# Two transformer blocks in one Trainium2 kernel: feed-forward columns of both token streams joined, attention heads paired, projections reordered, and the last layer's norm taken in token blocks

## The chip, the cores and the metric

The kernel runs on one core of one Trainium2 chip. The metric is the device time of one execution in microseconds (us), as the median over several runs. A TensorE matmul instruction here multiplies a stationary tile (loaded by a weight load) with a moving tile of up to 512 columns; VectorE (DVE), ScalarE (ACT) and GpSimd (POOL) do everything else, and SyncE (SP) issues most transfers.

## The reference

The input is 256 tokens of width 1024, and a context of another 256 tokens. A first block of two layers runs on the tokens alone (retention and stick-breaking attention, then a gated feed-forward with 2816 hidden columns). A second block of two layers runs on both, with shared weights:

```python
x = first_block(x, ...)
h = ctx
for l in range(2):
    x = ffn_sublayer(x, mod_x, 0, *f0)      # adaptive norm, swiglu, adaptive norm, residual
    h = ffn_sublayer(h, mod_h, 0, *f0)      # the same weights
    ax, ah = adaln_in(x, ...), adaln_in(h, ...)
    uv, qb, qc, kb, vb, kc, vc = split(ax @ w_in[l])   # for ah too; in the last layer only kb, vb, kc, vc
    o_a = chunk_gmlp(uv, ...)                          # gated token mixing
    o_b = diff_attention(qb, [kb_h, kb_x], [vb_h, vb_x])   # 4 heads, two softmaxes each
    o_c = windowed_attention(qc, kc, vc, kc_h, vc_h, sink) # 4 heads on 2 key heads
    x = adaln_out(x, concat(o_a, o_b, o_c) @ w_out[l], ...)   # h too, but not in the last layer
    x = ffn_sublayer(x, mod_x, 2, *f1)                        # h too, but not in the last layer
return x
```

Everything is float32. The modulation vectors mod_x and mod_h come from a product with w_mod (1024 x 9216 per layer).

## The kernel before

**Products in three passes.** A float32 product is made from two halves: a value is split into a high part, rounded to a shorter format (fp32r), and the rest, its low part. A product is high x high + high x low + low x high, three matmuls. A weight granule of 1024 columns per partition comes by DMA into a `raw` tile; `split` writes its high part on ScalarE (`A.copy`) and its low part on VectorE (`V.tensor_sub`), in two pieces each, into an `hl` tile, of which there are five. The activations' parts are tiles `y` (before a projection), `a` (inside the feed-forward) and `o` (the mixer's output), high part written by ScalarE, low part by VectorE after it. `mm3` issues the three matmuls of one contraction step next to each other, and `proj` calls it for each of the eight steps of a column pair.

**Streams and a planner.** The program is a list of units in five streams: `sx` (the tokens, called X), `sh` (the context, H), `sat` (attention), `smod` (modulation vectors on VectorE) and `stot`. `run` is a planner at build time: it picks, by costs and classes in tables (`PE_NS`, `CLASS`), which unit's instructions are emitted next, so the order on each engine's queue is fixed when the kernel is built, and each engine executes its queue in order.

**Feed-forward.** `ffn` has 22 columns j of 128 hidden units. `col(j)` makes gate and up of one column for one stream in one bank of PSUM (tile `mm_c`, 48 matmuls of 256 moving columns, one for each pass, step and matrix), then SiLU, product and split. `row(s)` multiplies two hidden columns with w_down into 1024 outputs (24 matmuls of 512 columns; tile `mm_r` where H adds in SBUF, `mm_f` where X keeps sums in PSUM). In block 2 the streams X and H run beside each other and share most weight granules; each has its own `col`.

**Mixer of block 2.** `attn2` makes the projections (`kb0`, `kb1`, `vb`, `kcvc`, `v`, `qb0`, `u`, `qb1`, `qc`, in this order) and the attention items: for each differential head and each half of the tokens two score matmuls (`at_s`), softmax (VectorE maximum, ScalarE exponential, VectorE scaling of `p`), transposes (`at_t`) and a value product (`at_o`); the windowed heads have one score matmul for each item on 64 rows of the array (`v` selects the rows) and a value product `at_c` on 64 output columns. `bapply` and `gm` finish the mixer's parts, and `row_units` multiplies with w_out. `post_units` adds to the residual (`res`) what was scaled by an inverse root mean square, `pre_units` normalises (`z`), transposes (`mm_y`) and writes `y`. Nearly every instruction is recorded at the helper's line 205, so the rows below are told apart by their tiles.

## Time and profile before

| | |
|---|---|
| median of 3 runs | 2468.3 us (2467.7 to 2470.83) |
| the profiled execution | 2468.97 us, of which the profile's span is 2467.1 us |
| TensorE | 2409.6 us busy (98%), 16543 matmuls, mean granted clock 0.993 |
| VectorE, ScalarE | 1727.6 us (70%), 1094.3 us (44%) |
| chain that ended last | TensorE 88%, VectorE 8% |

A busy TensorE is not TensorE at its peak: the end of a matmul in the profile is modelled, and a group's time is best read from the start of one group to the start of the next. A granted clock of 1.00 is 2.4 GHz and of 0.50 is 1.2 GHz; values between are a mix over the stretch.

### The profile page before, as it was taken

The page shows a single profiled execution, that of the slowest core. Times are in us where ns is not written, and L with a number is a line of the kernel's source. Part 1 is how long each engine was busy: PE and PEld are TensorE (multiplying, and loading weights), DVE is VectorE, ACT ScalarE, POOL GpSimd, SP SyncE. Part 2 cuts the span into 40 slices and gives each one's busy share as a digit, 9 for nine tenths or more (in the row PEclk, how much of TensorE's full clock was granted, in tenths as well). Part 3 has the DMA queues.
Part 4 walks back from the last instruction along what each step waited for, and adds up shares of the span by engine and source line. Part 5 has one row for each costly group of instructions (what it writes and reads, how often), then busy time and mean ns, then how long its engine had stood idle before and what let it go on. Part 6 is the DMA issues. An engine that isn't in the chain of part 4 may idle for free.

```text
span 2467.1 us, 41782 instructions
## 1 busy us (share of the span) xinstructions
PE 2409.6 (98%) x16543; PEld 2211.5 (90%) x16543; DVE 1727.6 (70%) x3366; ACT 1094.3 (44%) x2331; POOL 99.3 (4%) x189
## 2 busy tenths in 40 slices
PE   8999999999999999999999999999999999997998
PEld 7999999999999999989669999999999999866997
DVE  5789667798789933756688994348998448486554
ACT  6654456545532222636465222236322226465443
POOL 1000000010011000000000100000110000000000
PEclk9999999999999999999999999999999999999999
DMA  7568655686667533522226652245675335322663
GB/s 228 165 209 263 179 168 158 191 267 194 205 188 210 167 98 90 178 88 84 62 94 205 214 180 86 86 120 188 206 213 154 95 87 181 93 86 78 190 193 120
DMA packets 455301, 386.26 MB, mean 157 GB/s; under 512 B 20512, under 2 KB 380260, under 8 KB 455104
## 3 DMA queue, kind: packets, MB, share of 16 engines
q1 hardware_dynamic: 431280, 299.67, 41.0%
q0 software_dynamic: 23648, 83.77, 10.7%
q8 instruction: 130, 2.13, 0.4%
q14 instruction: 67, 0.55, 0.1%
q10 hardware_dynamic: 176, 0.14, 0.0%
HBM read 382.43 MB, written 1.10 MB: 155 GB/s over the span
## 4 chain that ended last, share of the span: by engine, by line
PE 88%; DVE 8%; ACT 1%; DMA 1%; issue 1%; DVEq 0%; ACTq 0%
PE mm_c L205 57%; PE mm_f L205 17%; PE mm_r L205 6%; DVE hl L205 2%; PE at_s L205 2%; PE mm_t L205 1%; DVE res L205 1%; PE at_o L205 1%; DVE fo L205 1%; PE at_t L205 1%; DMA raw<-in_w_in_dram 1%; DVE t L205 1%; PE at_c L205 1%; PE st_rb L205 1%; DVE rs_t L205 1%
## 5 line engine op out<-in xcount | busy, mean ns | idle before, releaser
L205 PE MATMUL mm_c<-y,hl 128*128 128x256 f32 x11616 | 1436.4, 284 | 10.4 <-DVE y L205 7.5
L205 PEld LDWEIGHTS mm_c<-y,hl 128*128 128x128 f32 x11616 | 1418.8, 192 | 23.8 <-DVE y L205 8.8
L205 ACT CAST hl<-raw 128x512 fp32r<-128x512 f32 x1128 | 649.0, 619 | 814.5 <-PE mm_c L205 445.3
L205 DVE TENSOR_TENSOR hl<-raw,hl 128x512 fp32r<-128x512 f32 x1128 | 733.2, 685 | 339.4 <-ACT hl L205 338.3
L205 PE MATMUL mm_f<-hl,a 128*128 128x512 f32 x1584 | 381.5, 393 | 0.0
L205 PEld LDWEIGHTS mm_f<-hl,a 128*128 128x128 f32 x1584 | 291.5, 188 | 57.6
L205 DVE SCALAR_TENSOR_TENSOR modacc<-modraw,sc,modacc 128x1024 f32<-128x1024 f32 x252 | 311.6, 1277 | 0.0
L205 ACT ACTIVATE sg<-mm_c 128x256 f32<-128x256 f32 x154 | 58.6, 381 | 311.0 <-PE mm_c L205 307.5
L205 PE MATMUL mm_r<-hl,a 128*128 128x512 f32 x792 | 190.5, 392 | 0.0
L205 DVE TENSOR_TENSOR sg<-sg,mm_c 128x256 f32<-128x256 f32 x154 | 64.0, 416 | 154.0 <-ACT sg L205 153.2
L205 PEld LDWEIGHTS mm_r<-hl,a 128*128 128x128 f32 x792 | 145.2, 188 | 28.0
L205 PE MATMUL mm_f<-hl,o 128*128 128x512 f32 x480 | 119.3, 399 | 0.0
L1000 POOL DMA_DIRECT2D modraw<-in_w_mod_dram x144 | 77.3, 538 | 991.6 <-DVE modacc L205 625.8
L205 PE MATMUL mm_c<-hl,y 128*128 128x512 f32 (+1 forms) x528 | 108.7, 363 | 0.0
L205 PEld LDWEIGHTS mm_f<-hl,o 128*128 128x128 f32 x480 | 87.8, 189 | 23.1 <-issue 4.6
L205 PEld LDWEIGHTS mm_c<-hl,y 128*128 128x128 f32 x528 | 88.8, 189 | 14.7 <-issue 0.3
L205 DVE TENSOR_TENSOR fo<-fo,mm_r 128x512 f32<-128x512 f32 x120 | 81.6, 682 | 9.2 <-PE mm_r L205 8.5
L205 ACT CAST a<-sg 128x256 fp32r<-128x256 f32 x154 | 62.5, 406 | 30.1 <-DVE sg L205 30.0
L205 DVE TENSOR_TENSOR a<-sg,a 128x256 fp32r<-128x256 f32 x154 | 64.4, 418 | 8.5 <-ACT a L205 8.5
L205 DVE TENSOR_TENSOR gu<-mm_c,rfac 128x512 f32<-128x512 f32 x44 | 30.3, 688 | 48.7 <-PE mm_c L205 48.6
L205 DVE TENSOR_REDUCE sx<-at_s 128x1 f32<-128x512 f32 (+1 forms) x72 | 40.8, 596 | 26.3 <-PE at_s L205 25.7
L205 DVE TENSOR_REDUCE modt<-mm_t 128x4 f32<-128x512 f32 x72 | 49.2, 684 | 8.4 <-PE mm_t L205 8.2
(196 smaller groups left out, 1412.4 us busy)
## 6 DMA issues: line engine op xcount, KB each, us to landing
modraw<-in_w_mod_dram POOLq DMA_DIRECT2D x144, 512.0 KB, 4.7
raw<-in_ffn_w_down_dram SPq DMA_DIRECT2D x100, 512.0 KB, 4.4
raw<-in_ffn_w_gate_dram SPq DMA_DIRECT2D x98, 512.0 KB, 4.7
raw<-in_ffn_w_up_dram SPq DMA_DIRECT2D x98, 512.0 KB, 3.9
raw<-in_w_in_dram SPq DMA_DIRECT2D x92, 512.0 KB, 4.7
raw<-in_w_gate_dram SPq DMA_DIRECT2D x44, 512.0 KB, 4.9
raw<-in_w_up_dram SPq DMA_DIRECT2D x44, 512.0 KB, 5.1
raw<-in_w_down_dram SPq DMA_DIRECT2D x44, 512.0 KB, 4.9
```

What stands on the lines that cost most here:

```text
L205: return f(*args, **kw)
L1000: G.dma_start(M["raw"][g % len(M["raw"])], wm[k * P:(k + 1) * P, i * D:(i + 1) * D])
```

## The change

1. **Joint columns.** In the two feed-forwards of block 2's first layer and in the first one of its last layer, columns 2 to 19 (first feed-forward) or 4 to 19 (second) are made for both streams at once: `both(j)` has a unit for gate and one for up, each with 24 matmuls whose moving operand is `yy[:, :, part, k, :]`, 2 x 256 columns in two runs. `y`, and the mixer's output, now lie in one tile `yy` for both streams. That is 52 columns.
2. **Paired heads.** A windowed-attention item now takes two heads (`v` = 0 and 1) that lie on different 64 rows of the array in the scores and on different 64 output columns in the value product, whose matmuls alternate. w_out's rows for this part are loaded in a matching order.
3. **Mixer reordered.** The projections' order is the table `SEQ`; `bapply` and `gm` have places of their own, `gm` now after the last attention item; w_out's parts come as 1, 2, 3, 0; more buffers for transposed weights (`wt`, 4).
4. **Low part last.** `proj` now makes three passes over the steps: high x high, weights' low x high, and the activations' low part last.
5. **Last layer by token blocks.** The last two parts of w_out run for token block 0 and then for block 1; norm, residual and `z` are made for each block by itself, the gate is multiplied into a tile `fg` beside the squares (`beside`), and the first four weight granules of the last feed-forward get their low part on GpSimd (`by_pool`).
6. Modulation in block 1 uses the buffers of block 2's (`mod_buf2`), and the scratch for GpSimd's transfers is set to 8192.

```diff
+SEQ = ("kb0 kb1 qb0 vb qb1 kcvc qc v u".split(),
+           "kb0 kb1 vb qb0 qb1 kcvc qc v u".split())
...
+    PASSES = ((0, 0), (1, 0), (0, 1))
...
     def proj(ps, gs, y, ks=range(KT)):
-        for k in ks:
-            for m, g in enumerate(gs):
-                mm3(ps[:, m, :], wsl(g, 0, k, 0, P), wsl(g, 1, k, 0, P), y[:, 0, k, :], y[:, 1, k, :],
-                    k == 0 and m == 0, k == KT - 1 and m == 1)
+        for wp, yp in PASSES:
+            for k in ks:
+                for m, g in enumerate(gs):
+                    PE.matmul(ps[:, m, :], wsl(g, wp, k, 0, P), y[:, yp, k, :],
+                              start=k == 0 and m == 0 and wp + yp == 0, stop=k == KT - 1 and m == 1 and yp == 1)
...
+        def both(j):
+            box = {}
+            def part(g, ps):
+                for wp, yp in PASSES:
+                    for k in range(KT):
+                        PE.matmul(ps, wsl(g, wp, k, 0, P), yy[:, :, yp, k, :],
+                                  start=k == 0 and wp + yp == 0, stop=k == KT - 1 and yp == 1)
...
+            ug = st.add("joint", gate, grans=[gg[j]], deps=dep if j == 0 else ())
+            cols[j] = joint[1][j] = st.add("joint", up, grans=[gu[j]])
...
                     yield A
+                    if beside:
+                        if gated[0] is None:
+                            gated[0] = wk.tile([P, 2, D], F32, tag="A1", name="fg")
+                        def mul():
+                            yield V
+                            fo[c][b][e] = gated[0][:, b, e * 512:(e + 1) * 512]
+                            V.tensor_mul(fo[c][b][e], f, ctab[c][:, e * 512:(e + 1) * 512])
+                        meter.spawn(mul())
                     sq_piece(c, b, e, f)
...
+        for g in range(2):
+            for b in range(2):
+                def sc(g=g, b=b):
+                    pt = ptile()
+                    pss = [at_ps([P, 512], "at_s") for _ in range(2)]
+                    for v in range(2):
+                        PE.matmul(pss[v][:, :n], B["qc"][v * 64:v * 64 + 64, g, b * P:(b + 1) * P],
                                   K2["kc"][v * 64:v * 64 + 64, 0:n], start=True, stop=True)
...
+                    for j in range(nk):
+                        for v in range(2):
+                            PE.matmul(ps[v * 64:v * 64 + 64, :S], K2["vc"][:, j, v * 64:v * 64 + 64],
+                                      B["wtc", g][v][:, j, :], start=(j == 0), stop=(j == nk - 1))
...
+        pieces = (1, 2, 3, 0) if GM_AT[l] >= 12 else (1, 2, 0, 3)
...
+            for i in range(N_POOL):
+                for part in f1[:2]:
+                    part[i].by_pool = True
...
+            for n_ in range(4 - 2 if last else 4):
+                u = piece(n_)
+            for b in range(2 if last else 0):
+                for n_ in range(4 - 2, 4):
+                    u = piece(n_, (b,))
...
-        yield V
-        V.tensor_sub(g.hl[:, 1, c], r[:, c], g.hl[:, 0, c])
+        yield GP if g.by_pool else V
+        (GP if g.by_pool else V).tensor_sub(g.hl[:, 1, c], r[:, c], g.hl[:, 0, c])
```

On TensorE, in the second feed-forward of block 2's first layer, the queue before has two columns of one stream (`y_13964` is X's input, `y_13452` H's; `a_13667` and `a_14155` are the hidden columns of H and X), then rows, then a column of the other.

```order
L205 MATMUL mm_r<-hl,a_13667 128x512 x12
L205 MATMUL mm_c<-y_13964,hl 128x256 x96
L205 MATMUL mm_r<-hl,a_13667 128x512 x12
L205 MATMUL mm_f<-hl,a_14155 128x512 x6
L205 MATMUL mm_c<-y_13452,hl 128x256 x48
L205 MATMUL mm_f<-hl,a_14155 128x512 x18
L205 MATMUL mm_c<-y_13452,hl 128x256 x48
```

The same place in the changed kernel, where `yy` is the input of both streams and `a_12732` and `a_13210` are H's and X's hidden columns:

```order
L210 MATMUL mm_r<-hl,a_12732 128x512 x24
L210 MATMUL mm_c<-yy,hl 128x512 x24
L210 MATMUL mm_f<-hl,a_13210 128x512 x24
L210 MATMUL mm_c<-yy,hl 128x512 x72
L210 MATMUL mm_r<-hl,a_12732 128x512 x24
```

Two columns of both streams were 192 matmuls of 256 columns and are now 96 of 512; the rows are the same in number. Over the whole program 4,992 matmuls of 256 columns are replaced by 2,496 of 512.

On TensorE, where the last layer's attention of X begins before (`k_21693` are keys, `at_21912` holds the queries, `kr` and `at_r` the rotation of a projection):

```order
L205 MATMUL at_s<-k_21693,at_21912 128x512 x4
L205 MATMUL mm_c<-y_21857,hl 128x256 x48
L205 MATMUL at_s<-k_21693,at_21912 128x512 x2
L205 MATMUL at_t<-cst,p 128x128 x4
L205 MATMUL at_s<-k_21693,at_21912 128x512 x2
L205 MATMUL mm_c<-y_21857,hl 128x256 x24
L205 MATMUL at_t<-cst,p 128x128 x4
L205 MATMUL at_r<-kr,tab_c_6411 128x256 x4
L205 MATMUL at_s<-k_21693,at_21912 128x512 x2
L205 MATMUL at_t<-cst,p 128x128 x4
```

And in the changed kernel:

```order
L210 MATMUL at_s<-k_19011,at_19237 128x512 x4
L210 MATMUL mm_c<-yy,hl 128x256 x24
L210 MATMUL at_r<-kr,tab_c_6412 128x256 x2
L210 MATMUL at_s<-k_19011,at_19237 128x512 x2
L210 MATMUL mm_c<-yy,hl 128x256 x24
L210 MATMUL at_t<-cst,p 128x128 x4
L210 MATMUL at_s<-k_19011,at_19237 128x512 x2
L210 MATMUL mm_c<-yy,hl 128x256 x24
L210 MATMUL at_t<-cst,p 128x128 x4
```

Between the first scores and the last transposes there were 72 projection matmuls (`mm_c`, 256 columns) and 18 of w_out (`mm_f`, 512 columns); now there are 168 and none, and all 96 of w_out come after the attention.

On VectorE, at the norm between the last mixer and the last feed-forward, the queue before adds to the residual for both blocks and has four weight pieces (`hl`) between:

```order
L205 SCALAR_TENSOR_TENSOR rs_t<-rs_a,rs_t 128x2
L205 SCALAR_TENSOR_TENSOR res_78<-mm_f,rs_t,res_78 128x512 x3
L205 TENSOR_TENSOR hl<-raw,hl 128x512 x2
L205 SCALAR_TENSOR_TENSOR res_78<-mm_f,rs_t,res_78 128x512
L205 TENSOR_TENSOR hl<-raw,hl 128x512 x2
L205 SCALAR_TENSOR_TENSOR rs_v<-ssq 128x1 x2
L205 TENSOR_SCALAR rs_t<-rs_v 128x2
```

In the changed kernel, from token block 0's residual to block 1's:

```order
L210 SCALAR_TENSOR_TENSOR res_78<-fg,rs_t,res_78 128x512 x2
L210 TENSOR_TENSOR fg<-mm_f,coef_19197 128x512 x2
L210 SCALAR_TENSOR_TENSOR rs_v<-ssq 128x1
L210 TENSOR_SCALAR rs_t<-rs_v 128x1
L210 SCALAR_TENSOR_TENSOR rs_v<-ssq 128x1
L210 TENSOR_SCALAR rs_t<-rs_v 128x1
L210 SCALAR_TENSOR_TENSOR rs_t<-rs_t,rs_v 128x1
L210 TENSOR_TENSOR rs_a<-rs_t 128x1
```

Block 0's residual now stands ahead of block 1's chain of small steps, the weight pieces are gone from between, and both chains alternate.

## Rows read from the trace of the kernel before

**Rows 1.** The chain that ended last, shares of the span by engine.

```profile
PE 88%; DVE 8%; ACT 1%; DMA 1%; issue 1%; DVEq 0%; ACTq 0%
```

**Rows 2.** Timeline of TensorE, first layer's second feed-forward: start us, us, instruction, count.

```profile
1354.04 5.63 PE L205 MATMUL mm_r<-hl,a 128*128 128x512 f32 x24
1359.51 5.92 PE L205 MATMUL mm_c<-y,hl 128*128 128x256 f32 x48
1365.26 2.91 PE L205 MATMUL mm_f<-hl,a 128*128 128x512 f32 x12
```

**Rows 3.** Groups of instructions, shapes apart: count, busy us, mean ns.

```profile
L205 PE MATMUL mm_c<-y,hl 128*128 128x256 f32 x11616 | 1436.4, 284 | 10.4 <-DVE y L205 7.5 <-ACT hl L205 1.4 <-DVE t L205 1.1
```

**Rows 4.** Timeline of TensorE in the last layer's attention of X.

```profile
2198.48 1.13 PE L205 MATMUL at_s<-k,at 64*128 64x512 f32 x4
2199.54 0.66 PE L205 MATMUL at_t<-cst,p 128*128 128x128 f32 x4
...
2218.08 1.12 PE L205 MATMUL at_s<-kc,at 64*128 64x512 f32 x2
2219.14 0.66 PE L205 MATMUL at_t<-cst,p 128*128 128x128 f32 x4
...
2221.51 1.09 PE L205 MATMUL at_g<-ws,bt 128*64 128x128 f32 x16
2222.53 1.12 PE L205 MATMUL at_s<-kc,at 64*128 64x512 f32 x2
...
2236.96 1.94 PE L205 MATMUL at_c<-wtc,vc 128*64 128x256 f32 x8
2238.83 17.97 PE L205 MATMUL mm_f<-hl,o 128*128 128x512 f32 x78
```

**Rows 5.** Windows: length, then busy us of PE, PEld, DVE, ACT, POOL, granted clock.

```profile
1126.00:1206.00 80.00, 74.22 (x527) 63.93 (x525) 50.73 (x152) 43.09 (x109) 0.00 (x0) 0.96 0.22 67
1206.00:1288.00 82.00, 79.40 (x369) 50.49 (x369) 66.01 (x184) 54.38 (x139) 2.65 (x5) 0.97 0.28 87
2171.00:2233.00 62.00, 55.40 (x296) 36.48 (x294) 52.31 (x140) 36.86 (x94) 0.00 (x0) 0.97 0.16 52
2256.00:2277.00 21.00, 10.48 (x67) 9.90 (x66) 15.50 (x48) 10.81 (x27) 0.55 (x1) 0.76 0.26 83
1330.00:1343.00 13.00, 9.89 (x61) 9.70 (x60) 13.00 (x28) 5.93 (x14) 1.57 (x3) 0.74 0.71 220
```

**Rows 6.** Waits of TensorE: us in total, times, longest.

```profile
PE mm_y L205 <- DVE z L205: 13.9, 4, 10.5
PE mm_c L205 <- DVE y L205: 7.5, 7, 3.1
```

**Rows 7.** Timeline of VectorE and TensorE, norm ahead of the last feed-forward.

```profile
2257.64 0.69 DVE L205 TENSOR_TENSOR mm_f<-mm_f,coef 128x512 f32<-128x512 f32 x1
...
2259.80 2.07 DVE L205 SCALAR_TENSOR_TENSOR res<-mm_f,rs_t,res 128x512 f32<-128x512 f32 x3
...
2261.79 1.28 DVE L205 TENSOR_TENSOR hl<-raw,hl 128x512 fp32r<-128x512 f32 x2
...
2267.32 3.77 PE L205 MATMUL mm_y<-cst,z 128*128 128x128 f32 x16 [10.52 <-DVE z L205]
2270.74 4.50 PE L205 MATMUL mm_c<-y,hl 128*128 128x256 f32 x31
```

**Rows 8.** Timeline of TensorE, start of X's second feed-forward, first layer.

```profile
1329.06 1.91 PE L205 MATMUL mm_y<-cst,z 128*128 128x128 f32 x16
1330.72 0.36 PE L205 MATMUL mm_c<-y,hl 128*128 128x256 f32 x1
1334.19 20.02 PE L205 MATMUL mm_c<-y,hl 128*128 128x256 f32 x143 [3.10 <-DVE y L205]
```

**Rows 9.** Timeline of VectorE, the last norm.

```profile
2459.88 0.69 DVE L205 TENSOR_TENSOR mm_f<-mm_f,coef 128x512 f32<-128x512 f32 x1
...
2461.91 2.06 DVE L205 SCALAR_TENSOR_TENSOR res<-mm_f,rs_t,res 128x512 f32<-128x512 f32 x3
```

More of the change, by code (lines that the diff above doesn't have):

```diff
@@ L47 @@
 CLS_A = 1
-GM_AT = 11
+BA_AT = 9
+GM_AT = (12, 12)
 OWN_C = 2
@@ L53 @@
 OWN_B = 4
+N_POOL = 2
 MOD_LAT = 1000.0
@@ L625, in fn @@
                     yield V, of[b]
-                r = yield from rstd_tok(c, bs, Urgent if hard else Chained)
+                r = yield from rstd_tok(c, bs, Urgent if hard and 1 in bs else Chained)
                 if "z" not in box:
@@ L639, in head @@
             return fn
-        us = [st.add("head", head(bs), deps=deps) for bs in (((0,), (1,)) if of[0] is not of[1] else ((0, 1),))]
+        us = [(st, sat)[hard and bs == (0,)].add("head", head(bs), deps=deps)
+              for bs in (((0,), (1,)) if of[0] is not of[1] else ((0, 1),))]
         def tr(i):
@@ L676, in pre_units @@
         for i in range(4):
-            u = st.add("tr", tr(i), deps=d)
+            u = last_of[c] = st.add("tr", tr(i), deps=d)
             d = ()
@@ L742, in rest @@
                 def rest():
-                    if 1 in bs:
+                    if 1 in bs and not beside:
                         f = fo[c][1][1]
@@ L758, in post_units @@
         if apart:
-            us = [st.add("post", post((b,)), deps=[(d, 0.0)]) for b, d in enumerate((u_half[c], u))]
+            us = [(st, sat)[beside and b == 0].add("post", post((b,)), deps=[(d, 0.0)]) for b, d in enumerate((u_half[c], u))]
         else:
@@ L771, in coef_unit, with row_units @@
         st.add("none", fn, deps=[(mod_done[l, j], 0.0)])
-    def row_units(st, c, gp, src_of, first, last, mode, deps, by_token=True):
+    def row_units(st, c, gp, src_of, first, last, mode, deps, by_token=True, beside=False, bs=(0, 1)):
         u = None
+        gated = fgate[0] if 1 in bs and 0 not in bs else [None]
+        fgate[0] = gated
         order = ((0, 0), (0, 1), (1, 0), (1, 1)) if last and by_token else ((0, 0), (1, 0), (0, 1), (1, 1))
-        for n_, (b, e) in enumerate(order):
+        for n_, (b, e) in enumerate(o for o in order if o[0] in bs):
             def fn(b=b, e=e, n_=n_):
-                if first and n_ == 0:
+                if first and n_ == 0 and 0 in bs:
                     if mode == "sb":
@@ L869, in row @@
             return row_units(st, c, gd[s], src, s == 0, s == NJ // 2 - 1, mode,
-                             [(cols[2 * s + 1], 0.0)], by_token)
+                             [(cols[2 * s + 1], 0.0)], by_token, beside)
         for j in range(NJ):
-            col(j)
+            if joint is None or j not in joint[0]:
+                col(j)
+            elif c == H:
+                both(j)
+            else:
+                cols[j] = joint[1][j]
+                if j == joint[0][0]:
+                    joint[1]["first"].deps += ((last_of[X], 0.0),)
             if j >= 3 and j % 2 == 1:
-                row(j // 2 - 1)
+                u = row(j // 2 - 1)
+                if joint and c == X and j + 1 in joint[0]:
+                    joint[1][j + 1].deps += ((u, 0.0),)
         return row(NJ // 2 - 1)
@@ L1587, in uvu @@
             step("u", tail, 0)
-        roped("kb0", 5, lambda: K2["k"][:, 0:2, half], 1.0, 1, [dep] + ([(totals[l, 8], 0.0)] if c == H else kvdeps[:1]))
-        roped("kb1", 6, lambda: K2["k"][:, 2:4, half], 1.0, 1)
-        vb()
-        kcvc()
-        if kv_only:
-            flush()
-            return None, ev
-        if c == H or l == DEPTH - 1:
+        if not kv_only and (c == H or l == DEPTH - 1):
             def layer_consts():
@@ L1808, in attn2 @@
                 add_sc(i + DIST)
-            tu = sat.add("trp", items[i][3][1], deps=[(tv, 0.0)])
+            tu = sat.add("trp" if i < 8 else "trp2", items[i][3][1], deps=[(tv, 0.0)])
             todo, post = post, []
@@ L1833, in attn2 @@
                 last = f()
+        if GM_AT[l] >= len(items):
+            ug = sat.add("gm", gm, deps=[(ev["v"], 0.0), (ev["u"], 0.0), (uba, 0.0)])
         return {0: (ug, 0.0), 3: (last, 0.0), 1: (uba, 0.0), 2: (uba, 0.0)}, ev
@@ L1875, in tile_two_blocks @@
         go = [load_rows(io["w_out_2"][l], 4) for _ in range(2)]
+        for gp in go:
+            gp[3] = [Gran([io["w_out_2"][l][768 + P * v:768 + P * (v + 1), 512 * e:512 * (e + 1)].rearrange(
+                "(k p) n -> p k n", p=64) for v in range(2)], "row") for e in range(2)]
         f1 = (load_m(io["ffn_w_gate_2"][l, 1], NJ), load_m(io["ffn_w_up_2"][l, 1], NJ),
@@ L1887, in tile_two_blocks @@
             coef_unit(main, l, c, 0)
-            u = ffn(main, c, *ff[c][0], mode, [(u, L_TR)] + (dep[1] if c == H and l == 0 else []), pace.setdefault((l, c, 0), []))
+            u = ffn(main, c, *ff[c][0], mode, [(u, L_TR)] + (dep[1] if c == H and l == 0 else []), pace.setdefault((l, c, 0), []),
+                    joint=joints[0])
             if c == H:
@@ L1931, in load @@
             for e, ap in enumerate(g.ap):
-                nc.sync.dma_start(rv[:, :, 64 * e:64 * e + 64], ap)
+                half = slice(64 * e, 64 * e + 64)
+                nc.sync.dma_start(rv[half] if g.kind == "row" else rv[:, :, half], ap)
         else:
```

229 lines of the change are left out of this document (140 added, 89 removed).

## Prediction

> **What bounds the kernel now.** I read the chain that ended last first: 88% of the span is TensorE and nothing else reaches a tenth [rows 1]. So a term counts if it shortens TensorE's queue, or if it closes one of the few places where TensorE waits. Next the timeline of a feed-forward [rows 2]: groups follow each other without a gap, and the time from start to start is what a group costs. 24 matmuls of 512 columns take 1359.51 - 1354.04 = 5.47 us, 227.9 ns each; 48 of 256 columns take 1365.26 - 1359.51 = 5.75 us, 119.8 ns each. The mean of 284 ns in the groups [rows 3] is the latency of one among overlapping ones and prices nothing. Then the windows of the two attention stretches [rows 5]: there VectorE comes close to the wall, 52.3 of 62 us in the last layer and 66.0 of 82 us in the first layer's X, while the first layer's H stretch has it at 50.7 of 80. Last the waits [rows 6]: 13.9 us for `z`, of which 10.5 in one place, and 7.5 us in seven places for the low part of `y`.
>
> **Joint columns.** Two matmuls of 256 columns cost 2 x 119.8 = 239.6 ns, one of 512 costs 227.9 [rows 2], so each replaced pair gives 11.7 ns. 52 columns x 2 matrices x 24 = 2,496 pairs of the 11,616 small matmuls [rows 3]: 29.1 us. These stretches are TensorE's alone in the chain, so all of it is on the path; with the shorter period the weight pieces' casts and subtractions are as many as before, and SiLU and products now run on 512 columns once instead of twice on 256. What no row shows is a moving operand in two runs of 256. Its cost is bounded by the contiguous 512 (227.9, all 29.1 us) and by two separate 256 (239.6, nothing); I take the first, since it is the row that agrees in width, type and bank.
>
> The Trainium skill, page "TensorE: Matmul & The Clock Gate", section "Wait — 56ns, not 53.3ns?", gives a warm matmul N columns / 2.4 GHz plus about 2.5 ns. By it a pair of 256 would cost only 2.5 ns more than one of 512, and the term would be 6.2 us and the time about 2433 us. The rows here show 13 to 15 ns above N / 2.4 GHz at both widths, so they speak against it.
>
> **Paired heads and the new order.** Scores of two heads on the two halves of the rows, as the differential items already do them, take 2199.54 - 2198.48 = 1.06 us; one windowed head alone takes the same 1.06 us [rows 4]. Eight of these become four pairs: 4.2 us less for each X attention, and 2.1 for H, which has half the keys. The value product of one head, eight matmuls on 64 output columns, takes 1.87 us, 0.91 ns per streamed column; the `at_g` group, which alternates between the two column halves, takes 1.02 us for 16 of 128, 0.50 ns per column [rows 4]. So alternating halves run side by side, and four products of 1.87 become two: 3.7 us for each X, 1.9 for H.
>
> That is TensorE's work; what of it lands is another matter, since VectorE's softmax work is the same. In the last layer VectorE fills 52.3 of the 62 us between first maximum and last `p`, and the new order puts more weight splits and rotations into that stretch; I expect its length to stay, and the paired heads alone to give nothing there. What shortens the path is work moved under it: projection matmuls inside go from 72 to 168, 96 x 119.8 ns = 11.5 us, and 18 matmuls of w_out go out, 18 x 227.9 ns = 4.1 us, so 7.4 us net. In the first layer's X stretch TensorE drops 7.9 us and VectorE has 16 us of room on average but not everywhere; I take 6. In H's stretch TensorE drops 4.0 us, and of the 80 - 74.2 = 5.8 us in which it idles I count half as filled by the projections that now come later: 6.9. Sum 20.3 us. Bounds: 4 (only H's work lands) and 32 (20.3 plus the idle 6.6 and 2.6 of the other two stretches and the other half of H's).
>
> **Low part last.** The first two passes need only the high part of `y`, which ScalarE writes. At X's second feed-forward TensorE waits 3.10 us for VectorE's low part while VectorE is busy 13.0 of 13 us with modulation [rows 5, 8]; and the next 143 matmuls take 1354.04 - 1334.19 = 19.85 us instead of 17.13, with a granted clock of 0.74 in that window, between 1.2 and 2.4 GHz, after the wait. Six of eight high parts are there at the time. I take 3 us of these 5.8. In the other waits of about 1 us ScalarE must still write all eight high parts before the first pass ends, so little comes: 1 us in all. Sum 4, bounds 0 and 7.5 + 2.7 = 10.2.
>
> **Norm in the last layer.** TensorE stands 10.52 us ahead of the last feed-forward [rows 7]. Of that, block 1's chain no longer holds the gating product (0.65), two of the four residual adds (2 x 0.69) and a pair of weight pieces (1.28; the other pair lay under a square): 3.3 us less. Another 0.2 comes from the high part going first. What is late next is block 1's own chain of squares and small steps, about 7 us, so the slow transposes after it (3.42 us from 2267.32 to 2270.74 against 1.66 in [rows 8], at a granted clock of 0.76 [rows 5]) stay slow. 3.5 us. The weight pieces cost VectorE nothing but stand on GpSimd now, of which the trace shows no arithmetic: between 0.64 us for each (VectorE's row) and four times that, 2.6. Their first four are wanted by the second pass, some 10 us after TensorE stops, and 4 x 2.6 = 10.4 us just fits with the start that they have; if not, the wait is short. I keep bounds of -7 (below) and 8.
>
> **Last norm.** The product with the final gate (0.69) and one of three residual adds (2.06 / 3) leave the end of the chain [rows 9]: 1.3 us, bounds 0 and 2.
>
> **Nothing** for the buffers of block 1's modulation (same number and order of reads, hidden under a feed-forward that TensorE fills), twelve more issues on SP, and GpSimd's scratch. If transfers of w_mod got slower, VectorE's modulation would end later under the same feed-forward.
>
> **Sum.** 29.1 + 20.3 + 4 + 3.5 + 1.3 = 58.2 us off the profiled execution's 2468.97: 2410.8. The median shown is 0.7 lower, so 2410 us, 2.4% faster.
>
> **Rivals.**
> - *VectorE holds the attention.* If softmax sets the length of all three stretches but H's, the mixer's term is 4 instead of 20.3: 2426 us. For it speaks VectorE's share; against it that moved projections lie outside the stretch in any case.
> - *The idle goes too.* If the projections fill every gap, the mixer gives 32 and low-part-last 10: 2392 us. Against it: the last windowed items still stand alone in the queue.
> - *The fixed cost stays.* If a moving operand of two runs costs as much as two matmuls, the joint term is 0: 2439 us. Nothing in the trace has such an operand. The formula of the Trainium skill's page "TensorE: Matmul & The Clock Gate", section "Wait — 56ns, not 53.3ns?", would leave a weaker form of it, 2433 us.
> - *GpSimd gets in the way.* A GpSimd piece and a VectorE step could exclude each other. Eight pieces at 1.28 us, twice VectorE's, in turn with block 1's small steps would add up to 10.2 us to a chain that I shortened by 3.5: term -7, 2420 us. GpSimd does no arithmetic before, so no row bears on it. The Trainium skill, page "SBUF — State Buffer", section "SBUF: two separate sides", states such an exclusive lock for a VectorE instruction with two SBUF inputs against a GpSimd one; no run yet shows it.
> - *Slower than before.* If a moving operand of two runs cost more than two matmuls, each of the 2,496 would lose. The other terms give 29.1 us, 11.7 ns for each, so it decides from 239.6 + 11.7 = 251 ns. At the price of the dearest 512-wide row here, a score matmul at 1.06 / 4 = 265 ns, the time is 2410 + 2,496 x (265 - 227.9) ns = 2503 us. Against it: width and bank are those of the cheap row.
>
> **How the numbers follow.** Chances: forecast 0.57, VectorE holds the attention 0.13, idle goes too 0.11, fixed cost stays 0.08, GpSimd 0.06, slower 0.05. The forecast's own range is 2398 to 2422. To leave out no more than 2 in 10 I reach to just below the second rival and most of the way to the third: 2390 to 2434. About 0.2% (5 us) is what a measurement of this kernel can tell from no change; every case but the last is faster by more, and the last passes through no change, so faster 0.95, same 0.01, slower 0.04.
>
> **What would show it.** Right: a group of 24 joint matmuls from start to start in 5.47 us, two columns with their rows in 32.8 us instead of 34.0; `at_c` in groups of 16 at about 1.9 us; the wait for `z` ahead of the last feed-forward near 7 us; VectorE over 90% busy in the last layer's softmax stretch, about as long as now. Wrong: joint groups at 5.7 us or more; TensorE waiting in the joint columns for weight pieces or for X's `y`, which H did not need before; the last norm as long as now with GpSimd busy through it.

## The result and the profile after

The changed kernel takes 2409.01 us (median of 4 runs, 2407.21 to 2411.21) against 2469.57 us for the kernel before on the same chip: ratio 0.9755, 95% interval 0.9739 to 0.9772. The forecast was 2410. The profiled execution took 2411.21 us, with this on its page:

```profile
span 2409.4 us, 36677 instructions
PE 2358.2 (98%) x14047; PEld 2073.6 (86%) x14047; DVE 1723.7 (72%) x3322; ACT 1077.8 (45%) x2271; POOL 113.8 (5%) x197
PE 39%; DVE 6%; ACT 1%; issue 1%; DMA 0%; DVEq 0%; ACTq 0%
```

The third line is the chain [rows 1]. Its shares add up to 47% here, so the view didn't follow the chain to its start, and it can't be set beside the 88% of before. What can be compared in every profile of this kernel is when TensorE starts the transposes `mm_y` that open each stage. From one such start to a later one:

| stretch | before, us | after, us | saved | my terms for it |
|---|---|---|---|---|
| start and first block, to block 2's first `mm_y` | 673.0 | 678.5 | -5.5 | about 0 |
| first feed-forwards, layer 0 | 388.7 | 378.1 | 10.6 | joint 10.1 |
| mixers of H and X, layer 0 | 267.4 | 240.0 | 27.4 | 12.9 |
| second feed-forwards, layer 0 | 380.4 | 369.5 | 10.9 | joint 9.0, low part 3 |
| first feed-forwards, last layer | 389.0 | 379.3 | 9.7 | joint 10.1 |
| mixer and norm, last layer | 168.8 | 164.0 | 4.8 | 7.4 + 3.5 |
| last feed-forward and last norm | 199.8 | 200.0 | -0.2 | 1.3 |
| span | 2467.1 | 2409.4 | 57.7 | 58.2 with 1 us spread over the stages |

The row of the last layer's mixer holds the wait ahead of the last feed-forward, 10.5 us before and 15.1 after. The sum is right, several of its parts are not. What follows are the rows that answer to those of before.

Joint columns [rows 2, 3], TensorE's timeline (start us, us, instruction, count) and the groups by shape (busy us, mean ns):

```profile
1563.04 5.60 PE L210 MATMUL mm_r<-hl,a 128*128 128x512 f32 x24
1568.48 5.60 PE L210 MATMUL mm_c<-yy,hl 128*128 128x512 f32 x24
1573.92 5.60 PE L210 MATMUL mm_f<-hl,a 128*128 128x512 f32 x24
```

```profile
L210 PE MATMUL mm_c<-yy,hl 128*128 128x256 f32 x6624 | 828.1, 285 | 5.4 <-ACT yy L210 2.3 <-ACT hl L210 1.9 <-DVE t L210 1.3
L210 PE MATMUL mm_c<-yy,hl 128*128 128x512 f32 x2496 | 582.8, 391 | 0.0
```

A group of 24 joint matmuls takes 1573.92 - 1568.48 = 5.44 us, 226.7 ns each, as much as the group ahead of it (1568.48 - 1563.04), whose operand is contiguous. The 2,496 of them never wait (0.0 in the last column).

The value product of two heads [rows 4], then the stretches of the mixers [rows 5]: layer 0's H and X from first score to last value product, and the last layer's X from first maximum to last `p` (length, busy us of PE, PEld, DVE, ACT, POOL, granted clock):

```profile
2165.75 1.97 PE L210 MATMUL at_c<-wtc,vc 128*64 128x256 f32 x16
2167.64 1.09 PE L210 MATMUL at_t<-cst,p 128*128 128x128 f32 x8
```

```profile
1076.41:1185.93 109.52, 109.52 (x772) 97.74 (x771) 62.72 (x182) 50.68 (x134) 0.00 (x0) 1.00 0.24 68
1189.95:1249.07 59.12, 58.52 (x313) 39.96 (x313) 56.08 (x156) 45.20 (x113) 2.82 (x5) 1.00 0.32 103
2105.82:2166.27 60.45, 56.38 (x350) 43.58 (x348) 55.52 (x156) 44.11 (x103) 0.00 (x0) 0.94 0.25 78
```

16 matmuls take 1.89 us, where 8 took 1.87. In the last layer VectorE is busy for 55.52 of 60.45 us, 92%; before, the same stretch had 60.6 us (2171.95 to 2232.59). In layer 0 TensorE works through H's stretch without a pause and at the full clock.

TensorE's waits [rows 6], and X's second feed-forward in layer 0 [rows 8]:

```profile
PE mm_y L210 <- DVE z L210: 18.5, 4, 15.1
PE st_rb L210 <- DVE rs_t L210: 7.0, 2, 4.5
PE mm_c L210 <- ACT yy L210: 2.3, 3, 1.5
```

```profile
1296.62 1.91 PE L210 MATMUL mm_y<-cst,z 128*128 128x128 f32 x16
1298.28 2.66 PE L210 MATMUL mm_c<-yy,hl 128*128 128x256 f32 x12
1302.45 17.51 PE L210 MATMUL mm_c<-yy,hl 128*128 128x256 f32 x132 [1.51 <-ACT yy L210]
1319.80 3.14 PE L210 MATMUL mm_r<-hl,a 128*128 128x512 f32 x13
```

The wait for VectorE's low part is gone and ScalarE's high part is waited for instead. From `mm_y` to the rows behind the 144 matmuls it takes 23.2 us (1319.80 - 1296.62) instead of 25.0.

The norm ahead of the last feed-forward [rows 7], the timeline of VectorE and GpSimd, and TensorE's start behind it:

```profile
2190.80 0.16 DVE L210 TENSOR_TENSOR rs_a<-rs_t 128x1 f32<-128x1 f32 x1
2190.96 5.00 POOL L210 TENSOR_TENSOR hl<-raw,hl 128x512 fp32r<-128x512 f32 x4 [4.26 <-ACT hl L210]
2190.99 1.28 DVE L210 SCALAR_TENSOR_TENSOR rs_t<-rs_a,rs_t 128x2 f32<-128x2 f32 x1
2192.31 1.21 DVE L210 TENSOR_TENSOR rs_a<-rs_t 128x1 f32<-128x1 f32 x1
...
2194.80 1.18 DVE L210 TENSOR_TENSOR rs_a<-rs_t 128x1 f32<-128x1 f32 x1
2196.02 0.16 DVE L210 SCALAR_TENSOR_TENSOR rs_t<-rs_a,rs_t 128x1 f32<-128x1 f32 x1
...
2200.06 2.49 POOL L210 TENSOR_TENSOR hl<-raw,hl 128x512 fp32r<-128x512 f32 x2 [4.10 <-ACT hl L210]
2200.12 1.23 DVE L210 SCALAR_TENSOR_TENSOR rs_v<-ssq 128x1 f32<-128x1 f32 x1
2201.38 0.15 DVE L210 TENSOR_SCALAR rs_t<-rs_v 128x1 int32<-128x1 int32 x1
2201.45 1.11 DVE L210 SCALAR_TENSOR_TENSOR rs_v<-ssq 128x1 f32<-128x1 f32 x1
...
2209.39 3.65 PE L210 MATMUL mm_y<-cst,z 128*128 128x128 f32 x16 [15.09 <-DVE z L210]
```

TensorE waits 15.09 us instead of 10.52. Six of VectorE's steps on one or two elements, 0.16 us by themselves, take 1.1 to 1.3 us while GpSimd subtracts weight pieces of 1.25 us each (5.00 / 4), and each ends when a piece ends: 6.3 us lost in all.

The end [rows 9]:

```profile
2400.49 1.41 DVE L210 SCALAR_TENSOR_TENSOR res<-fg,rs_t,res 128x512 f32<-128x512 f32 x2
2401.82 1.28 DVE L210 TENSOR_TENSOR fg<-mm_f,coef 128x512 f32<-128x512 f32 x2
...
2404.75 1.42 DVE L210 SCALAR_TENSOR_TENSOR res<-fg,rs_t,res 128x512 f32<-128x512 f32 x2
```

Block 1's products with the gate still stand in the chain, now behind block 0's residual adds.

### The profile page after: what moved, and what is told of

Same layout as the page of the kernel before. It is cut to its first block, busy times and chain, and to the rows that moved or that the text cites. A ratio compares the mean times of both kernels' runs of the same rounds, so it can differ in the third digit from the quotient of the medians.

```text
span 2409.4 us, 36677 instructions
## 1 busy us (share of the span) xinstructions
PE 2358.2 (98%) x14047; PEld 2073.6 (86%) x14047; DVE 1723.7 (72%) x3322; ACT 1077.8 (45%) x2271; POOL 113.8 (5%) x197
## 5 line engine op out<-in xcount | busy, mean ns | idle before, releaser
L210 PE MATMUL mm_c<-yy,hl 128*128 128x256 f32 (+1 forms) x9120 | 1409.8, 314 | 5.4 <-ACT yy L210 2.3
L210 PEld LDWEIGHTS mm_c<-yy,hl 128*128 128x128 f32 x9120 | 1277.9, 191 | 115.7 <-ACT yy L210 5.9
L210 PE MATMUL mm_r<-hl,a 128*128 128x512 f32 x792 | 185.0, 390 | 0.7 <-DVE hl L210 0.7
L210 ACT ACTIVATE sg<-mm_c 128x256 f32<-128x256 f32 (+1 forms) x102 | 50.0, 490 | 254.7 <-PE mm_c L210 251.1
L210 DVE TENSOR_TENSOR sg<-sg,mm_c 128x256 f32<-128x256 f32 (+1 forms) x102 | 56.4, 552 | 118.6 <-PE mm_c L210 95.6
L210 PE MATMUL mm_f<-hl,yy 128*128 128x512 f32 x480 | 117.4, 397 | 0.0
L210 PE MATMUL mm_c<-hl,yy 128*128 128x512 f32 (+1 forms) x528 | 109.4, 364 | 0.0
L210 PEld LDWEIGHTS mm_f<-hl,yy 128*128 128x128 f32 x480 | 88.0, 188 | 20.8 <-issue 1.9
L210 PEld LDWEIGHTS mm_c<-hl,yy 128*128 128x128 f32 x528 | 89.0, 189 | 15.2 <-ACT hl L210 0.3
L210 DVE TENSOR_REDUCE modt<-mm_t 128x4 f32<-128x512 f32 x72 | 49.3, 685 | 19.1 <-PE mm_t L210 18.9
```

The source lines that it names most:

```text
L210: return f(*args, **kw)
```

## The experiments

Each ran against the kernel before on the same chip, whose medians there were 2469.3 to 2470.2 us, so times of different groups can be compared to about 2 us. Stretches are read between `mm_y` starts as above.

**1. No pieces on GpSimd.**

```diff
-N_POOL = 2
+N_POOL = 0
```

> The first weight pieces of the last feed-forward are subtracted by VectorE again instead of GpSimd (N_POOL = 0); all else as in the changed kernel. Theory (VectorE's small steps stand still while a GpSimd piece runs: 0.16 us became 1.2 us in six places): the small steps ahead of the last feed-forward go back to 0.16 us, TensorE's wait there falls from 15.1 us to 9 to 11 us, and the time is 2403 to 2406 us, 3 to 6 us below the changed kernel. Rival (the wait is long because block 1's squares stand behind block 0's residual in ScalarE's queue, GpSimd only happens to run then): steps stay long or the wait stays within 1 us of 15, time 2407 to 2411.

Measured: 2406.27 us (ratio 0.9743, 0.9728 to 0.9757). VectorE and TensorE at the same place:

```profile
2189.24 0.16 DVE L210 TENSOR_TENSOR rs_a<-rs_t 128x1 f32<-128x1 f32 x1
...
2198.21 1.89 DVE L210 TENSOR_TENSOR hl<-raw,hl 128x512 fp32r<-128x512 f32 x3
...
2204.59 3.65 PE L210 MATMUL mm_y<-cst,z 128*128 128x128 f32 x16 [11.84 <-DVE z L210]
```

All small steps are back at 0.16 us. The wait is 11.84 us, a little more than the 9 to 11 expected, since VectorE's own pieces, three of them in a row at 2198.21, now stand in the chain. The time, at 2406.27, is a hair above the theory's range. GpSimd's pieces held VectorE up: they are worth 3.25 us of the wait, and the rival, which had them do nothing, is out. That the wait is still longer than the 10.52 us of before is left to experiments 6, 8 and 11.

**2. Low part beside the others again.**

```diff
-        for wp, yp in PASSES:
-            for k in ks:
-                for m, g in enumerate(gs):
-                    PE.matmul(ps[:, m, :], wsl(g, wp, k, 0, P), y[:, yp, k, :],
-                              start=k == 0 and m == 0 and wp + yp == 0, stop=k == KT - 1 and m == 1 and yp == 1)
+        for k in ks:
+            for m, g in enumerate(gs):
+                mm3(ps[:, m, :], wsl(g, 0, k, 0, P), wsl(g, 1, k, 0, P), y[:, 0, k, :], y[:, 1, k, :],
+                    k == 0 and m == 0, k == KT - 1 and m == 1)
```

> The projections and single columns issue the three products of a contraction step next to each other again (low part not last); joint columns keep their passes. Theory A (passes over all eight steps hold a weight tile to its last third, so that in the first block, where columns are short of weights, each restart of TensorE is later): the 5.5 us that the changed kernel loses in the first block come back, and X's second feed-forward in the first layer starts about 1.5 us slower: in all 2 to 5 us faster than the changed kernel, 2404 to 2408. Theory B (the loss comes from the buffers of the first block's modulation or from the start of the transfers): the first block's landmarks stay within 1 us of the changed kernel and 1 to 4 us are lost at the starts of the feed-forwards: 2410 to 2414.

Measured: 2408.32 us (0.9749, 0.9734 to 0.9763), 0.7 us less than the changed kernel. The first block gets 4.6 us back (673.9 instead of 678.5), where theory A had 5.5; the second block gives 3.3 us of it away (1156.1 instead of 1152.8 us from X's `mm_y` ahead of layer 0's mixer to the last layer's `mm_y`). So the term is about zero, made of two that are not. Over the mixers alone the low part last gives 0.8 us in each layer (layer 0 takes 240.8 us here, the last layer 149.7 without its wait). Theory A's reason (weights held to their last third) is put to the test in experiment 12.

**3. No joint columns.**

```diff
-                    joint=joints[0])
+                    joint=None)
...
-                    joint=None if last else joints[1], beside=last)
+                    joint=None, beside=last)
```

> No joint columns: each stream makes its own gate and up with 256 columns, in the three feed-forwards too. Theory (2 x 119.8 against 226.7 to 227.9 ns, TensorE the only bound there): slower than the changed kernel by 2,496 x 11.7 to 12.9 ns = 29 to 32 us, that is 2438 to 2442 us. Rival (part of the 31 us of those three stages came from the passes or the order of columns, not from the width): slower by less than 24 us, 2425 to 2434.

Measured: 2440.91 us (0.9885, 0.987 to 0.99), 31.9 us slower. 31.9 / 2,496 = 12.8 ns for each pair; the rows give 2 x 119.8 - 226.7 = 12.9. By stage, from one `mm_y` start to the next, the three feed-forwards lose 10.9, 10.1 and 9.6 us, 30.6 in all, so the loss lies where the joint columns were. Theory confirmed.

**4. Single heads in the new order.** The items of one head each, as before, with four transposed-weight buffers, gating after the last item. (`bapply` keeps its number, 9, which with single heads is one head earlier.)

```diff
-        for g in range(2):
-            for b in range(2):
+        for v in range(2):
+            for g in range(2):
+                for b in range(2):
...
-GM_AT = (12, 12)
+GM_AT = (16, 16)
```

> The windowed heads are single again, eight items of one head instead of four of two, value products on 64 output columns one after the other; the projections' order, the places of the mixer's last parts and the rest stay as changed. Theory (in the last layer softmax on VectorE sets the stretch, in the first layer TensorE does): the first layer's mixers lose 7.9 + 4.0 = 12 us, give or take 2, the last layer's 0 to 3; 2421 to 2426 us. Rival 1 (TensorE's work counts in the last layer too): 18 to 21 us slower, 2427 to 2430. Rival 2 (the new order alone fills the gaps, the paired heads add little): less than 6 us slower, 2409 to 2415.

Measured: 2435.76 us (0.986, 0.9843 to 0.9876), 26.7 us slower, more than any of the three had: 19.1 us in layer 0 and 6.3 in the last layer, where TensorE's work counts too, as rival 1 had it.

**5. Old order, heads paired.** With `GM_AT` at 9 the gating stands ahead of the last two items, and w_out's parts come as 1, 2, 0, 3 again.

```diff
-    SEQ = ("kb0 kb1 qb0 vb qb1 kcvc qc v u".split(),
-           "kb0 kb1 vb qb0 qb1 kcvc qc v u".split())
+    SEQ = 2 * ("kb0 kb1 vb kcvc v qb0 u qb1 qc".split(),)
...
-GM_AT = (12, 12)
+GM_AT = (9, 9)
```

> The mixer's projections and last parts in the order of before (kb0 kb1 vb kcvc v qb0 u qb1 qc; gating before the last attention items; w_out's parts as 1, 2, 0, 3), the paired heads kept. Theory (the two parts add up: the single heads in the new order left 8.3 us of layer 0's mixers and 3.1 us of the last layer's): 9 to 13 us slower than the changed kernel, 2418 to 2422 us. Rival 1 (paired heads alone close the gaps): less than 5 us slower, 2409 to 2414. Rival 2 (each needs the other): more than 15 us slower, 2424 or more.

Measured: 2440.04 us (0.9879, 0.9865 to 0.9892), 31.0 us slower: rival 2. X's stretch in layer 0 (as the windows above), and TensorE near its end:

```profile
1202.44:1271.52 69.08, 61.16 (x327) 41.30 (x325) 62.96 (x179) 49.15 (x126) 2.86 (x5) 0.93 0.32 100
```

```profile
1252.62 1.09 PE L210 MATMUL at_g<-ws,bt 128*64 128x128 f32 x16
1261.18 1.94 PE L210 MATMUL at_t<-cst,p 128*128 128x128 f32 x8 [7.46 <-DVE sx L210]
```

The paired heads took work off TensorE, and it stands for VectorE's softmax instead: the gating product is done, the next group in its queue is the transposes of `p`, and 7.46 us pass until VectorE has made it. The clock falls with the wait, as a window of 4 us in which the wait begins and one behind it show (granted clock third from the end):

```profile
1252.00:1256.00 4.00, 1.72 (x23) 1.35 (x21) 4.00 (x13) 1.62 (x3) 2.09 (x4) 1.00 0.62 154
1262.00:1266.00 4.00, 4.00 (x20) 2.43 (x20) 3.66 (x15) 2.41 (x5) 0.77 (x1) 0.50 0.81 193
```

TensorE works at 2.4 GHz until it waits and at 1.2 GHz in the window behind the wait; over the stretch the mean is 0.93, where the changed kernel has 1.00.

**9 and 10. Half of the order each.** Experiment 9 has the changed kernel's projections and the old place of gating and w_out's parts, experiment 10 the reverse.

```diff
-GM_AT = (12, 12)
+GM_AT = (9, 9)
```

> The changed kernel with its order of projections, but the gating product ahead of the last attention items again and w_out's parts as 1, 2, 0, 3. Theory (the projections that are left until the heads' softmax runs are what TensorE works on meanwhile; the place of the last parts is minor): 2 to 8 us slower than the changed kernel, 2411 to 2417 us. Rival (the gating product and its part of w_out are what was missing at the end of the stretch): 15 us slower or more, 2424 us or more.

```diff
-    SEQ = ("kb0 kb1 qb0 vb qb1 kcvc qc v u".split(),
-           "kb0 kb1 vb qb0 qb1 kcvc qc v u".split())
+    SEQ = 2 * ("kb0 kb1 vb kcvc v qb0 u qb1 qc".split(),)
```

> The changed kernel with the order of projections of before (kb0 kb1 vb kcvc v qb0 u qb1 qc), the gating product after the last attention item and w_out's parts as 1, 2, 3, 0 as changed. Theory: most of the 31 us that the old order costs stays, 2428 to 2437 us, with TensorE waiting for VectorE's softmax. Rival: most comes back, 2410 to 2420 us.

Measured: 2425.86 us (0.9826, 0.9813 to 0.984) and 2421.39 us (0.9808, 0.9794 to 0.9821). My theory that the projections do most of it is wrong: 16.9 us are lost without the new place of the last parts, which was the rival of experiment 9, and 12.4 without the new projections, which is between the theory and the rival of experiment 10. X's stretch in experiments 9 and 10:

```profile
1193.68:1263.83 70.15, 62.88 (x323) 43.56 (x322) 61.95 (x178) 49.94 (x126) 2.79 (x5) 0.93 0.35 113
```

```profile
1197.78:1258.15 60.37, 59.29 (x313) 40.40 (x313) 54.84 (x151) 42.83 (x109) 2.62 (x5) 1.00 0.22 69
```

The place of the last parts closes X's stretch (70.2 to 60.4 us); the projections' order closes H's: from X's `mm_y` ahead of the mixer to H's `mm_y` behind it 204.1 us in experiment 9 and 203.0 in the changed kernel, against 212.3 and 211.0 in experiments 5 and 10. All mixers together (layer 0 from X's `mm_y` ahead of the mixer to the one behind it, the last layer the same without the wait ahead of its last feed-forward):

| heads | projections | last parts | layer 0, us | last layer, us | |
|---|---|---|---|---|---|
| single | old | old | 267.4 | 158.3 | before |
| paired | old | old | 262.0 | 157.4 | 5 |
| single | new | new | 259.1 | 155.2 | 4 |
| paired | new | old | 252.7 | 152.2 | 9 |
| paired | old | new | 249.7 | 151.7 | 10 |
| paired | new | new | 240.0 | 148.9 | after |

Paired heads alone give 6.3 us, the order alone 11.4, both 36.8: more than half of the gain (19.1 us) comes only when both are there. The row of before also lacks the low part last, 0.8 us for each layer by experiment 2, so the two single gains are if anything smaller. Where the 19.1 us lie can be read from TensorE's busy time (the first figure behind the length) in layer 0's mixers: before, experiment 5 (paired, old order), experiment 4 (single, new order), after.

```profile
1061.70:1329.10 267.40, 257.98 (x1599) 211.24 (x1600) 174.87 (x470) 149.70 (x352) 2.65 (x5) 0.98 0.30 90
1054.40:1316.40 262.00, 246.00 (x1595) 207.84 (x1596) 174.17 (x470) 146.68 (x346) 2.86 (x5) 0.96 0.31 91
1055.30:1314.40 259.10, 253.22 (x1595) 208.86 (x1596) 173.83 (x470) 145.16 (x347) 2.81 (x5) 1.00 0.31 92
1056.60:1296.60 240.00, 239.38 (x1594) 204.05 (x1595) 171.21 (x470) 140.05 (x341) 2.82 (x5) 1.00 0.33 99
```

TensorE stands idle for 9.4, 16.0, 5.9 and 0.6 us of these. Pairing takes 12.0 us of work from TensorE in the old order and 13.8 in the new. In the old order 6.6 us of them come back as idle time; in the new order the idle time shrinks by 5.3 besides. In the last layer's mixer, without its wait, the idle times are 7.6, 11.8, 4.6 and 4.3 us.

**6. Norm of the last layer for both blocks at once,** no pieces on GpSimd.

```diff
-                return row_units(main, c, go[c][i], src, n_ == 0, n_ == 3, "ps", [od[i]], True, last, bs)
+                return row_units(main, c, go[c][i], src, n_ == 0, n_ == 3, "ps", [od[i]], True, False, bs)
...
-            for n_ in range(4 - 2 if last else 4):
+            for n_ in range(4):
...
-            u = post_units(main, c, "ps", u, last, False, last, last)
+            u = post_units(main, c, "ps", u, False, False, last)
```

> The norm ahead of the last feed-forward is taken for both token blocks at once, as in the kernel before (w_out's last parts not by blocks, gate multiplied in place), and the weight pieces are VectorE's; so it differs from the run without GpSimd by the token blocks of that norm alone. Theory (with the pieces on VectorE the token blocks shorten nothing, since pieces and the other block's steps stand inside each block's chain): TensorE waits 10 to 11 us there instead of 11.8, and the time is 2404 to 2407 us. Rival (token blocks are worth the 3.5 us that I had forecast, GpSimd alone spoiled them): the wait is 14 us or more, 2408 to 2411.

Measured: 2404.46 us (0.9739, 0.9725 to 0.9752). TensorE waits 9.3 us, less than the 10 to 11 expected and 2.5 less than with token blocks in experiment 1. The theory, that token blocks shorten nothing, holds; with pieces in the chain they even cost.

**7. Both losses taken back:** N_POOL = 0, and the first block's `proj` with `mm3`.

```diff
+        if beside:
+            for k in ks:
+                for m, g in enumerate(gs):
+                    mm3(ps[:, m, :], wsl(g, 0, k, 0, P), wsl(g, 1, k, 0, P), y[:, 0, k, :], y[:, 1, k, :],
+                        k == 0 and m == 0, k == KT - 1 and m == 1)
+            return
...
-                proj(ps, (gg[j], gu[j]), y)
+                proj(ps, (gg[j], gu[j]), y, beside=joint is None and not beside)
```

> No pieces on GpSimd, and the low part beside the others in the first block alone (passes stay in the second block). Theory (the two losses are apart and each can be had back): the first block's 4.6 us and the norm's 2.7 us both come back, 2401 to 2403 us, faster than both kernels. Rival (the first block's start only moves a wait on to the next place): 2404 us or more.

Measured: 2403.23 us (0.9739, 0.9725 to 0.9752; five runs of 2401.99 to 2407.14). By the median it lies just above the theory's range; its profile (span 2400.2) has block 2's first `mm_y` at 672.8, and block 2, from X's `mm_y` ahead of layer 0's mixer to the last layer's `mm_y`, takes 1149.8 us as in experiment 1 (1149.7). So both losses come back; the runs lie 5 us apart, and the time itself settles less than these starts.

**8. Pieces held until `z` is made.** As experiment 7, and the planner skips VectorE's weight pieces until `z` of both blocks is made.

```diff
         for x in tails:
+            if x.unit is None and x.eng == "v" and held:
+                continue
...
-            held = False
+            n_go += 1
+            held = n_go < 2
...
-        us[-1].lets_go = hard
+        for x in us:
+            x.lets_go = hard
```

> As the run before it, and the planner lets no weight piece's subtraction into VectorE's queue from the last w_out matmuls until both blocks' z are made; five pieces stand behind z then. Theory (five to eight pieces of 0.69 us inside the chain of the norm are what keeps TensorE waiting 11.8 us): the wait falls to 8 or 9 us, 2398 to 2400 us. Rival (the low parts then come too late for the first column, so TensorE waits there instead): within 1.5 us of the run before it.

Measured: 2400.48 us (0.9721, 0.9708 to 0.9734).

```profile
2198.81 3.09 DVE L210 TENSOR_TENSOR hl<-raw,hl 128x512 fp32r<-128x512 f32 x5
2199.04 3.46 PE L210 MATMUL mm_y<-cst,z 128*128 128x128 f32 x16 [8.82 <-DVE z L210]
...
2202.26 4.02 PE L210 MATMUL mm_c<-yy,hl 128*128 128x256 f32 x31
```

The five pieces stand behind `z`, the wait is 8.82 us, and the first column doesn't wait for them. The wait fell as expected, by 3.0 us from experiment 7's 11.85; the time is half a microsecond above its range.

**11. As 8, norm for both blocks at once** (its diff is that of experiment 6, with the pieces held until `z`).

> As the run with the held pieces (2400.5 us; no GpSimd, low part beside in the first block, pieces held until z), but the norm ahead of the last feed-forward for both token blocks at once. Theory (token blocks by themselves shorten that wait by no more than 1 us): TensorE waits 8 to 10 us there, 2399 to 2402 us. Rival (token blocks are worth 3 us or more once nothing stands in their chain): a wait of 12 us or more, 2403 us or more.

Measured: 2400.3 us (0.9725, 0.9712 to 0.9738), wait 9.0 us. So the token blocks of that norm are worth 0.2 us of the wait and nothing in the time.

**12. Two passes.** As experiment 8, but every `proj` in two passes, also in the first block: in the first both parts of the weights meet the high part of `y`, four matmuls for a step, in the second comes the low part of `y`.

```diff
-        for wp, yp in PASSES:
-            for k in ks:
+        for yp in range(2):
+            for k in ks:
+                for wp in range(2 - yp):
...
```

> As the run with the held pieces, but every projection and single column in two passes: in the first both parts of the weights with the high part of y, four matmuls for a step (0.48 us), in the second the low part of y. Theory (three passes lose at a norm because two matmuls for a step, 0.24 us, ask for y's parts faster than ScalarE writes them, 0.47 us each; four do not): from the second to the sixth start of the first block 529.0 us, give or take 0.5, as with the parts beside, and not 531.3; in the second block the gain of the low part last stays; 2399 to 2402 us. Rival (it is the weights, held or wanted otherwise by passes): 531 us or more, 2402 us or more.

Measured: 2398.87 us (0.9715, 0.9702 to 0.9728), the fastest of all. From the second `mm_y` start of the program to the sixth, block 2's first: 529.1 us (before 528.9, experiments 2, 7, 8 and 11 528.9 to 529.0, all with three passes 531.2 to 531.3). Block 2, measured as in experiment 7, takes 1143.6 us here and 1146.2 in experiment 8, so the gain of the low part last stays there. The first projection behind the second start in the changed kernel, with ScalarE's writes of `y`, then in this experiment, then in the kernel before:

```profile
149.12 0.62 ACT L210 ACTIVATE sq<-res 128x512 f32<-128x512 f32 x1
149.15 0.72 PE L210 MATMUL mm_c<-yy,hl 128*128 128x256 f32 x4
...
149.73 2.29 ACT L210 ACTIVATE yy<-mm_y,vecs 128x256 fp32r<-128x256 f32 x6
150.25 6.16 PE L210 MATMUL mm_c<-yy,hl 128*128 128x256 f32 x44 [0.38 <-ACT yy L210]
```

```profile
147.36 6.15 PE L210 MATMUL mm_c<-yy,hl 128*128 128x256 f32 x48
```

```profile
146.06 0.36 PE L205 MATMUL mm_c<-y,hl 128*128 128x256 f32 x1
...
146.70 5.88 PE L205 MATMUL mm_c<-y,hl 128*128 128x256 f32 x47 [0.28 <-DVE y L205]
```

With two matmuls for each step TensorE has caught up with ScalarE after the first two parts of `y`, waits, and runs the rest from a broken start; with four it runs through. Part of the gap is a square of the residual (`sq`, 0.62 us) that ScalarE makes between the second part and the third, in this experiment too; with four matmuls for a step TensorE is still at the first two steps then. The rate is the cause at the norms, and theory A's reason in experiment 2 (weights) is not: two passes still want the weights' high part to the end.

## Why the prediction was right, and where it was not

**The time** was right to 1 us, but not by its terms. By the table the mixers gave 16.5 us more than I had (36.8 for 20.3, the norm's wait left out) and the three feed-forward stages 2.1 more than the joint columns' 29.1; against that stand 8.1 in the norm, 5.5 in the first block, 4 for the low part and 1.5 at the end. That the time came out is luck: the errors cancel to half a microsecond.

**Joint columns: right, a little small.** 31.9 us (experiment 3) for 29.1; the operand in two runs costs 226.7 ns, what the contiguous one costs. "The fixed cost stays" and the slower rival are out. The 2.5 ns of the Trainium skill's page "TensorE: Matmul & The Clock Gate", section "Wait — 56ns, not 53.3ns?", do not price this kernel: by them the estimate was 6.2 us for this term, by the runs it is 31.9.

**Paired heads and order: mechanism half right in the last layer, wrong in layer 0.** I had written that the last layer's softmax stretch would keep its length with VectorE over 90% busy: 60.45 us and 92%. Paired heads alone give nothing there in the old order (0.9 us), as I had it, but 6.3 us in the new one; and the order, to which I gave all 7.4 us, gives 3.1 without the pairs (experiment 4) and 9.4 with them. In layer 0 the step that failed is "In the first layer's X stretch ... I take 6" and "half as filled" for H. The bound of 32 was too low as well (36.8). What the runs show in its place: of 9.4 us of idle time 8.8 went, where I took 2.9. The clock in those stretches was 0.96 and 0.97 before [rows 5] and 1.00 once the waits were gone, for which I had no term. And I priced pairing and order as a sum, while each needs the other: of the 13.7 us in layer 0 that come only with both (27.4 - 5.4 - 8.3), 11.8 are idle time and 1.9 busy time of TensorE by the four windows above; in the last layer 4.4 of 5.4 are idle time. So in layer 0 the rival "the idle goes too" was right in kind, but too small: by its sum layer 0 gives 18.4 us (12.9, X's idle 2.6, the other half of H's 2.9), and it gave 27.4.

**Low part last: wrong, about zero.** The gain at X's second feed-forward was 1.8 us instead of 3, and 3.3 for all of block 2. The failed step is "ScalarE must still write all eight high parts before the first pass ends, so little comes": it costs. Three passes ask ScalarE for a step's part every 0.24 us, and it writes one in about 0.4 (2.29 / 6 in the row above), while VectorE in the first block had kept up with `mm3`'s 0.72 but for one wait of 0.28 us (row of before above). That is 2.4 us over four norms of the first block (531.3 for 528.9). From the first `mm_y` to the second the profiles scatter: 136.6 to 139.6 us with the parts beside (five profiles, mean 137.9), 138.5 to 141.0 with three passes (eight, mean 139.8). By these means the passes cost some 1.9 us there too, but the two groups overlap and no run shows which step it would be; the remaining 1.2 of the 5.5 are within the scatter. I had called the buffers of the modulation and GpSimd's scratch nothing; they stay in experiments 2 and 7, which lose nothing, so that holds. They were not tried by themselves.

**Norm in the last layer: wrong in sign.** Forecast 3.5 us less, measured 4.6 more. Of my rivals "GpSimd gets in the way" came true; it had 10.2 us for eight pieces and the term at -7, and the six steps that met one lost 6.3 us. The Trainium skill's page "SBUF — State Buffer", section "SBUF: two separate sides", states that such a pair of instructions excludes each other for a whole instruction; the trace agrees: steps of 0.16 us with two SBUF inputs last as long as the GpSimd piece beside them, 1.1 to 1.3 us, and the one with a single input (2201.38, 0.15 us) doesn't. But the step was wrong without GpSimd too: 11.8 us with token blocks (experiment 1). Only with all pieces out of the chain does it come to 8.8, and then the norm for both blocks at once has 9.0 (experiments 8 and 11). What I had counted as leaving the chain, the gate's product and two adds of block 1, doesn't shorten the wait. By the order in the queues it is paid back by block 0's steps that stand between on VectorE and by block 0's squares ahead of block 1's on ScalarE; no run takes those away by themselves.

**Last norm: wrong, 0.5 us lost for 1.3 gained.** From the last matmul to the end it takes 9.3 us (2409.4 - 2400.1) instead of 8.8 (2467.1 - 2458.3); all twelve experiments, which keep this norm as changed, have 9.3 too. By the rows it is the same mistake, block 0's residual adds are ahead of block 1's products.

What stays open: the scatter of up to 3 us between starts of the program, and which step of the last layer's norm by token blocks pays back what the others save.

## What to carry to other kernels

Work that is taken off the busy engine and work that is moved into its waits are not two terms to be added: while another engine sets a stretch's length, the first only makes idle time, and the second needs that room. Moving a low part to the end of a product asks the engine that writes the high part for a higher rate, so compare matmuls for each step with that engine's time for a part (here four for a step were right, two were not). And before work is given to GpSimd, see which VectorE steps run at that time: a chain of tiny steps is what it hurts most.

## What was unexpected of the hardware

VectorE steps on one or two elements of each partition took 1.1 to 1.3 us beside a GpSimd subtraction of 128x512, seven to eight times their 0.16 us, six times over, and eight such pieces cost TensorE more waiting than the same pieces on VectorE at 0.69 us. TensorE went from 2.4 to 1.2 GHz with a wait of 7.46 us and worked at 1.2 GHz behind it, so such a wait costs more than its own length. And an operand of two runs of 256 columns cost 226.7 ns, nothing above a contiguous 512.
